# A decoder layer on one core: another order of the PSUM banks in the down projection, and a norm statistic and its squares moved in the opening

## The chip, the core and the metric

The kernel runs on one core of one Trainium2 chip. A core has a matrix engine (TensorE, PE in the profile, with its weight loads as PEld), a vector engine (VectorE, DVE), a scalar engine (ScalarE, ACT), a general engine (GpSimd, POOL) and a queue engine (SyncE, SP). Each engine takes its instructions in the order in which they stand in its queue. Matrix products are summed in PSUM, which has eight banks of 128 x 512 float32. The metric is the time of one execution on the device in microseconds (us).

## What is computed

One layer on x of 1024 tokens by 1024 features, all in float32:

```python
x = x + 0.5 * swiglu(rmsnorm(x, g1), gate1, up1, down1)   # (silu(h@gate) * (h@up)) @ down, width 2816
x = x + hybrid_mixer(rmsnorm(x, gm), ...)                 # gated linear attention and short convolutions
x = x + 0.5 * swiglu(rmsnorm(x, g2), gate2, up2, down2)
return rmsnorm(x, gf)
```

`rmsnorm` multiplies x by `rsqrt(mean(x*x) + eps)` and a gain.

## The kernel before

x lies in SBUF transposed: `xs[k]` holds 128 features by 1024 tokens, and the tokens are worked on in two halves of 512. Each float32 operand is split into a high and a low part (`split`: ScalarE casts, L92 or L557; VectorE subtracts, L85), and one product of two operands is three matrix instructions of 128 x 512, the `PASSES`. So "three instructions" below is one 128 x 128 block times 512 tokens.

Each SwiGLU (class `Ffn`) goes over 22 blocks of 128 of the inner width. `ups(f)` makes gate and up of block f for both halves at once by a seven product (Strassen) scheme; `down(g)` takes two such blocks, 2g and 2g+1, back to the 1024 features by seven products as well. The order of work is f = 4, 5, 6, ... with `down(g)` straight behind each even `ups(f)`, so a pair of `ups` with one `down` is 84 + 84 + 84 matrix instructions. There are 10 calls of `down` in each of the two SwiGLUs; the first call of the first one stands behind `ups(3)`, the 19 others behind an even `ups`.

PSUM banks are given out by number. An even `ups` uses banks 0 to 3 (`b = 4 * (f % 2)`): "a" is bank 0, "b" bank 1, "c" bank 2, "e" bank 3; an odd one uses banks 4 to 7. Bank 1 is read last by VectorE's product of silu(gate) and up (L701), bank 2 by ScalarE's silu of the last of the seven products (L705). `down` then writes its first product p = 1 for j = 0 to 3, three instructions each, into the four banks `a0[j]`, with copies by ScalarE into the banks `b0[j]` (L748):

```python
a0, b0 = [0, 3, 1, 2], [4, 7, 5, 6]
...
for j in range(4):
    if p == 1:
        av[j] = self.bank(a0[j])
        self.prod1(av[j], l4, r, True)
        bv[j] = self.bank(b0[j])
        S.copy(bv[j], av[j])
```

The last product of `down` (p = 4) sums into the same banks, and VectorE adds them to x for j = 0 to 3 (`xadd`, L715).

The first SwiGLU begins with `opening`, whose order is written by hand. `block(f, n, rights)` is gate and up of block f for half n, plain, in eight steps of six instructions; `some(b, m)` issues m steps of it. The first three blocks of half 0 are multiplied by x times gain, and the norm is applied after (`gated`: L536 and L537 on VectorE, silu L538 on ScalarE, L540 on VectorE). Half 1 is normed first. A `Norm` has `add(k)` (ScalarE squares x, L303, and VectorE adds to the sum, L88, one behind) and `fin`, a generator: its first `next` issues the statistic (L326: the sum times ones on TensorE, L337 on VectorE, a power L339 on GpSimd), its second the diagonal matrix `dg` (L343, VectorE), its third the broadcast by TensorE (L347) and ScalarE's copy of it to SBUF (`rb`, L351). `n0` and `n1` are the norms of the halves.

All instructions of a call keep the written order on TensorE; up to the first `down` they do so on all engines. Weights come by DMA from SP's queue some blocks ahead.

Of the kernel before, what the change touches and what calls it, by code (L numbers as in the profile page):

```python
# [19 lines left out]
KT = D // P  # L20
# [35 lines left out]
def trunk(ctx: ExitStack, tc: tile.TileContext, a, out):  # L56
# [22 lines left out]
    def t2(name):  # L79
        return room("t2", name)  # L80
# [6 lines left out]
    def add(eng, o, x, y):  # L87
        eng.tensor_tensor(o, x, y, op=ALU.add)  # L88
# [28 lines left out]
    def pump(n=None):  # L117
        while todo and n != 0:
            n = n and n - 1
            tag, step = todo[0]  # L120
            if not tag():
                return
            todo.popleft()
            step()

    def free(tag, n=1):
        used[tag] -= n
        assert used[tag] >= 0
# [116 lines left out]
    def tick(us):  # L245
        pump()
        clock[0] += us
        for e in list(later):
            if e[0] <= clock[0]:
                w = next(e[1], None)  # L250
                if w is None:
                    later.remove(e)
                else:
                    e[0] = clock[0] + w
# [16 lines left out]
    def xh(k, n):  # L271
        return xs[k][:, n * HALF:(n + 1) * HALF]
# [95 lines left out]
    def part_of(lt, j):  # L368
        return lt[:, j * P:(j + 1) * P], lt[:, 512 + j * P:512 + (j + 1) * P]
    class Ffn:  # L370
# [142 lines left out]
        def opening(self, n0, n1, load1):  # L513
# [7 lines left out]
            def some(b, n):  # L521
                for _ in range(n):
                    ps = next(b)
                return ps
# [7 lines left out]
            def gated(pss, n):  # L532

                o = t2("act")
                if n == 0:
                    V.tensor_tensor(o, pss[0], n0.r, op=ALU.mult)  # L536
                    V.tensor_tensor(pss[1], pss[1], n0.r, op=ALU.mult)  # L537
                S.activation(o, o if n == 0 else pss[0], AF.Silu)  # L538
                yield
                V.tensor_tensor(o, o, pss[1], op=ALU.mult)  # L540
                yield o
# [36 lines left out]
            a0 = self.block(0, 0, X)  # L578
# [9 lines left out]
            fin = n0.fin(self.bank_norm)  # L588
# [3 lines left out]
            some(a1, 2)  # L592
            n1.add(3)
            next(fin)
            n1.add(4)
            some(a1, 1)
            next(fin, None)
            for k in range(5, KT):
                n1.add(k)
            pump(6)  # L600
            act00 = gated(ps00, 0)
            next(act00)
            ps10 = some(a1, 2)
            fin = n1.fin(self.bank_norm)
            next(fin)
            act10 = gated(ps10, 0)
            a = [next(act00)]
            b = self.block(2, 0, X)
            some(b, 2)
            next(act10)  # L610
            next(fin)
            a.append(next(act10))
            some(b, 1)
            next(fin, None)
            ps20 = some(b, 5)

            self.right("R11", "R")
            for q in range(2):
# [115 lines left out]

        def down(self, g):

            a0, b0 = [0, 3, 1, 2], [4, 7, 5, 6]
            av, bv = {}, {}
            for n, p in enumerate(DOWN):
                lt, rt = self.left(("d", g), p), self.rights[n]  # L740
                r = [(rt[:, 0:512], rt[:, 512:1024])]
                for j in range(4):
                    l4 = part_of(lt, j)
# [5 lines that stand above are left out]
                    elif p == 2:  # L749
                        self.prod1(av[j], l4, r, False)  # L750
                        self.xadd(j, 0, av[j])
                    elif p == 6:
                        self.prod1(bv[j], l4, r, False)
                        av[j] = self.bank(a0[j])
                        S.copy(av[j], bv[j])
                    elif p == 3:
                        self.prod1(bv[j], l4, r, False)
                        self.xadd(4 + j, 0, bv[j])
                    elif p == 7:
                        self.prod1(av[j], l4, r, False)  # L760
                        self.xadd(4 + j, 1, av[j])
                    elif p == 5:
                        bv[j] = self.bank(b0[j])
                        self.prod1(bv[j], l4, r, True)
                        t = t2("dx")
                        S.mul(t, bv[j], 0.5)  # L766
                        for i in range(2):
                            add(G, xh(4 + j, i), xh(4 + j, i), t)
                    else:
                        self.prod1(av[j], l4, r, False)  # L770
                        self.xadd(j, 1, av[j])
                if n + 3 < len(DOWN):
                    self.rights[n + 3] = self.rights[n + 3]()
                free("wo")
                tick(2.72)
# [481 lines left out]
    n1 = [Norm(0, chain=V), Norm(HALF, chain=V)]  # L1257
# [200 lines left out]
```

## Time and profile before

| | |
|---|---|
| time, median of 3 executions | 1807.79 us (1807.17 to 1808.7) |
| the profiled execution's own time | 1805.88 us |
| its span in the profile | 1804.1 us |
| TensorE busy | 1741.6 us, 97% of the span |
| VectorE, ScalarE, GpSimd busy | 76%, 46%, 35% |
| mean granted TensorE clock | 0.986 |

The span reaches from the first to the last instruction of the profiled execution; 1.8 us of its time lie outside. The profiled execution was 1.9 us faster than the median of the three others. A granted clock of 1.00 is TensorE's level of 2.4 GHz, 0.50 that of 1.2 GHz.

### The profile page before, as it was taken

How to read it: one execution, taken by the hardware profiler on the slowest of the kernel's cores; microseconds unless marked ns; L12 is line 12 of the kernel's file. 1: busy time of each engine (PE TensorE's matmuls, PEld its weight loads, DVE VectorE, ACT ScalarE, POOL GpSimd, SP SyncE). 2: the span in 40 equal slices, each digit the busy share in tenths (PEclk: the TensorE clock that was granted, in tenths of full speed). 3: DMA queues.
4: the chain of work that ended last, by engine and by line, in shares of the span. 5: the costliest groups of instructions: out<-in, count | busy, mean ns of one | idle time of the engine just before them, and what ended most of it. 6: DMA issues, size and time to landing. Idle time of an engine off the chain costs nothing.

```text
span 1804.1 us, 21022 instructions
## 1 busy us (share of the span) xinstructions
PE 1741.6 (97%) x7814; PEld 1430.7 (79%) x7814; DVE 1373.1 (76%) x1847; ACT 831.0 (46%) x1442; POOL 627.6 (35%) x425
## 2 busy tenths in 40 slices
PE   8989999999999998899999999999999999999995
PEld 7768888888888875788888887888888888888884
DVE  6898778877798775775746678787788777977785
ACT  5465444554455444432352444454455544554453
POOL 0044254533444242220211021442545334442533
PEclk9999999999999998999999999999999999999997
DMA  5011212111111211222222223012121111112102
GB/s 213 1 47 47 71 47 71 47 48 62 55 47 47 71 53 47 82 82 82 72 92 83 82 71 101 17 36 70 48 70 48 47 60 58 47 47 70 47 24 94
DMA packets 35110, 112.92 MB, mean 63 GB/s; under 512 B 4384, under 2 KB 6848, under 8 KB 35008
## 3 DMA queue, kind: packets, MB, share of 16 engines
q1 hardware_dynamic: 32944, 108.42, 18.3%
q10 hardware_dynamic: 2064, 3.16, 0.5%
q8 instruction: 61, 1.00, 0.2%
q14 instruction: 41, 0.34, 0.1%
HBM read 107.37 MB, written 4.19 MB: 62 GB/s over the span
## 4 chain that ended last, share of the span: by engine, by line
PE 44%; issue 24%; POOL 17%; DVE 13%; ACT 2%; DMA 0%; POOLq 0%; ACTq 0%; DVEq 0%
PE ps L779 15%; POOL x L88 12%; PE pj L898 12%; PE dn L1203 5%; POOL raw L85 4%; DVE w L85 3%; PE ps L364 2%; PE v L953 2%; PE ps L799 2%; DVE S L85 2%; PE sc L1022 1%; DVE T L85 1%; DVE act L85 1%; PE ps L506 1%; DVE act L701 1%
## 5 line engine op out<-in xcount | busy, mean ns | idle before, releaser
L364 PE MATMUL ps<-R,w 128*128 128x512 f32 x1872 | 443.0, 390 | 3.4 <-DVE x L715 2.4
L364 PEld LDWEIGHTS ps<-R,w 128*128 128x128 f32 x1872 | 352.3, 188 | 77.9 <-DVE x L715 2.8
L779 PE MATMUL ps<-act,w 128*128 128x512 f32 x1680 | 390.0, 391 | 10.0 <-DVE act L701 9.3
L779 PEld LDWEIGHTS ps<-act,w 128*128 128x128 f32 x1680 | 313.7, 188 | 83.1 <-DVE act L701 17.3
L85 DVE TENSOR_TENSOR w<-raw,w 128x512 fp32r<-128x512 f32 x311 | 292.3, 946 | 78.8 <-ACT w L92 78.8
L364 PE MATMUL ps<-S,w 128*128 128x512 f32 x1404 | 331.3, 389 | 1.2 <-ACT w L92 1.2
L364 PEld LDWEIGHTS ps<-S,w 128*128 128x128 f32 x1404 | 263.4, 188 | 56.7 <-ACT w L92 1.7
L85 POOL TENSOR_TENSOR raw<-raw 128x512 f32<-128x512 f32 x59 | 77.3, 1310 | 608.0 <-DVE w L85 608.0
L88 POOL TENSOR_TENSOR x<-x,dx 128x512 f32<-128x512 f32 x160 | 265.7, 1697 | 17.4 <-ACT dx L766 17.4
L92 ACT CAST w<-raw 128x512 fp32r<-128x512 f32 x311 | 192.3, 620 | 167.3 <-POOL raw L85 75.9
L715 DVE SCALAR_TENSOR_TENSOR x<-ps,x 128x512 f32<-128x512 f32 x320 | 210.1, 682 | 33.7 <-PE ps L779 33.7
L898 PE MATMUL pj<-h,whi 128*128 128x512 f32 x640 | 200.4, 394 | 0.0
L85 DVE TENSOR_TENSOR wlo<-raw,whi 128x1024 fp32r<-128x1024 f32 x64 | 80.8, 1263 | 88.8 <-PE pj L898 47.4
L898 PEld LDWEIGHTS pj<-h,whi 128*128 128x128 f32 x640 | 118.9, 189 | 26.4 <-issue 1.9
L218 ACT CAST whi<-raw 128x1024 fp32r<-128x1024 f32 x64 | 67.0, 1047 | 138.7 <-PE pj L898 81.8
L85 DVE TENSOR_TENSOR w<-T,w 128x512 fp32r<-128x512 f32 x118 | 102.4, 868 | 37.1 <-ACT w L92 37.1
L898 PE MATMUL pj<-h,wlo 128*128 128x512 f32 x320 | 124.9, 390 | 0.0
L85 DVE TENSOR_TENSOR act<-act,act 128x512 fp32r<-128x512 f32 x103 | 109.9, 1069 | 13.1 <-ACT act L92 13.1
L92 ACT CAST act<-act 128x512 fp32r<-128x512 f32 x103 | 63.8, 622 | 75.1 <-PE ps L779 45.9
L92 ACT CAST w<-T 128x512 fp32r<-128x512 f32 x118 | 73.4, 622 | 53.5 <-PE ps L364 32.0
L85 POOL TENSOR_TENSOR raw<-raw,raw 128x512 f32<-128x512 f32 x59 | 95.6, 1620 | 4.6
L85 DVE TENSOR_TENSOR T<-raw,raw 128x512 f32<-128x512 f32 x59 | 49.6, 840 | 53.0 <-POOL raw L85 53.0
(196 smaller groups left out, 2150.7 us busy)
## 6 DMA issues: line engine op xcount, KB each, us to landing
raw<-in_ffn_w SPq DMA_DIRECT2D x86, 512.0 KB, 3.5
raw<-in_ffn_wd SPq DMA_DIRECT2D x44, 512.0 KB, 3.6
raw<-in_w_fm SPq DMA_DIRECT2D x40, 512.0 KB, 3.5
raw<-in_w_out SPq DMA_DIRECT2D x16, 512.0 KB, 3.5
x<-in_x SPq DMA_DIRECT2D x16, 256.0 KB, 6.4
raw<-in_w_v SPq DMA_DIRECT2D x8, 512.0 KB, 3.6
raw<-in_ffn_w ACTq DMA_DIRECT2D x2, 512.0 KB, 6.1
out<-y SPq DMA_DIRECT2D x2, 512.0 KB, 2.8
```

Of the source, the lines that this page charges most:

```text
L85: eng.tensor_tensor(o, x, y, op=ALU.subtract)
L88: eng.tensor_tensor(o, x, y, op=ALU.add)
L92: S.copy(hi, src)
L218: S.copy(st[1], st[0])
L364: nc.tensor.matmul(ps, lt[:, c:c + P], rk[j], start=(start and n == 0), stop=(n == last), skip_group_check=True)
L506: nc.tensor.matmul(pss[m], lts[m][:, c:c + P], rk[j], start=(q == 0 and k == 0 and t == 0), stop=(q == 1 and k == 3 and t == 2))
L715: V.scalar_tensor_tensor(xh(d, n), ps, 0.5, xh(d, n), op0=ALU.mult, op1=ALU.add)
L779: nc.tensor.matmul(ps, l2[i], r[0][j], start=(start and n == 0), stop=(n == 2), skip_group_check=True)
L799: nc.tensor.matmul(ps, l2[i], rts[h][q][:, 512 * j + o:512 * j + o + w], start=(q == 0 and k == 0), stop=(q == 1 and k == 2))
L898: nc.tensor.matmul(pss[f], w[i][:, k, f * P:(f + 1) * P], h[j][:, 4 * kh + k, :], start=(kh == 0 and k == 0 and n == 0), stop=(kh == 1 and ...
L953: nc.tensor.matmul(pss[t], h[i][:, kk, t * P:(t + 1) * P], u[j][:, k * 512:(k + 1) * 512], start=(kk == 0 and i == 0 and j == 0), stop=(kk ...
L1203: nc.tensor.matmul(pss[j], w[p][:, f * 512 + j * P:f * 512 + (j + 1) * P], act[q][i][:, f * 512:(f + 1) * 512], start=(i == 0 and f == 0 a ...
```

## The change

Two edits. `down` takes its four banks of gate and up in the order 0, 3, 2, 1. In the opening the squares 4 to 7 of half 1 are issued ahead of the broadcast of half 0's norm, the statistic of half 1 comes behind the first step of block 2 and behind the first `gated` result, and the broadcast of half 1 comes three steps before the end of block 2.

```diff
             next(fin)
-            n1.add(4)
+            for k in range(4, KT):
+                n1.add(k)
             some(a1, 1)
             next(fin, None)
-            for k in range(5, KT):
-                n1.add(k)
             pump(6)
             act00 = gated(ps00, 0)
             next(act00)
             ps10 = some(a1, 2)
-            fin = n1.fin(self.bank_norm)
-            next(fin)
             act10 = gated(ps10, 0)
             a = [next(act00)]
             b = self.block(2, 0, X)
+            some(b, 1)
+            fin = n1.fin(self.bank_norm)
+            next(fin)
             some(b, 2)
             next(act10)
             next(fin)
             a.append(next(act10))
-            some(b, 1)
+            some(b, 2)
             next(fin, None)
-            ps20 = some(b, 5)
+            ps20 = some(b, 3)
...
-            a0, b0 = [0, 3, 1, 2], [4, 7, 5, 6]
+            a0, b0 = [0, 3, 2, 1], [4, 7, 5, 6]
```

On TensorE, at the end of block 1 (`ps_229`, `ps_230`) and in block 2 (`ps_355`, `ps_356`), there stood before (a row is one instruction or several alike; `sq_116` is the sum of half 1's squares):

```order
L506 MATMUL ps_230<-S_4_114,S_16_224 128x512 x3
L326 MATMUL ps_345<-ones,sq_116 128x2 x4
L506 MATMUL ps_355<-S_3_113,L_319 128x512 x3
L506 MATMUL ps_356<-S_3_113,L_319 128x512 x3
L506 MATMUL ps_355<-S_3_113,L_319 128x512 x3
L506 MATMUL ps_356<-S_3_113,L_319 128x512 x3
L506 MATMUL ps_355<-S_3_113,L_319 128x512 x3
L506 MATMUL ps_356<-S_3_113,L_319 128x512 x3
L347 MATMUL ps_382<-dg_373,ones 128x512
```

At the same place of TensorE's queue stands now (block 2 is `ps_345`, `ps_346`):

```order
L506 MATMUL ps_230<-S_4_114,S_16_224 128x512 x3
L506 MATMUL ps_345<-S_3_113,L_319 128x512 x3
L506 MATMUL ps_346<-S_3_113,L_319 128x512 x3
L326 MATMUL ps_354<-ones,sq_116 128x2 x4
L506 MATMUL ps_345<-S_3_113,L_319 128x512 x3
L506 MATMUL ps_346<-S_3_113,L_319 128x512 x3
L506 MATMUL ps_345<-S_3_113,L_319 128x512 x3
L506 MATMUL ps_346<-S_3_113,L_319 128x512 x3
L506 MATMUL ps_345<-S_3_113,L_319 128x512 x3
L506 MATMUL ps_346<-S_3_113,L_319 128x512 x3
L506 MATMUL ps_345<-S_4_114,L_319 128x512 x3
L506 MATMUL ps_346<-S_4_114,L_319 128x512 x3
L347 MATMUL ps_394<-dg_379,ones 128x512
```

Six instructions of block 2 moved ahead of the statistic, and 24 instead of 18 stand between the statistic and the broadcast; 18 instead of 30 are left behind it. The profile counts twice as many instructions for L326 and L347, 8 and 2.

On ScalarE, around the copy `rb` of half 0's broadcast (`L_319` is block 2's weights):

```order
 L303 ACTIVATE sq_116<-x_82 128x512
-L351 COPY rb_307<-ps_305 128x512
 L303 ACTIVATE sq_116<-x_83 128x512
 L303 ACTIVATE sq_116<-x_84 128x512
 L303 ACTIVATE sq_116<-x_85 128x512
+L351 COPY rb_313<-ps_311 128x512
 L92 CAST L_319<-raw_315 128x512 x2
 L92 CAST L_319<-raw_317 128x512 x2
```

Three squares stand ahead of the copy now, and block 2's casts come right behind it. On VectorE the first `gated`'s L540 now stands ahead of the last addition to the sum (L88) instead of behind the statistic.

On TensorE, in the p = 1 of a `down` behind an even `ups` (`ps_1199` is j = 1, `ps_1205` j = 2, `ps_1211` j = 3), with what the first instruction of each group waits for:

```order
 L779 MATMUL ps_1199<-act_1110,w_1101 128x512 x3
-L779 MATMUL ps_1205<-act_1110,w_1101 128x512 [waits DVE_49]
+L779 MATMUL ps_1205<-act_1110,w_1101 128x512 [waits Activation_49]
 L779 MATMUL ps_1205<-act_1110,w_1101 128x512 x2
-L779 MATMUL ps_1211<-act_1110,w_1101 128x512 [waits Activation_49]
+L779 MATMUL ps_1211<-act_1110,w_1101 128x512 [waits DVE_49]
 L779 MATMUL ps_1211<-act_1110,w_1101 128x512 x2
```

The wait for VectorE moved from j = 2 to j = 3, and that for ScalarE from j = 3 to j = 2. SP's queue is the same, word for word.

## Rows read from the trace of the kernel before

**Rows 1.** The page: engine, busy us, share, instructions, for TensorE

```profile
PE 1741.6 (97%) x7814; PEld 1430.7 (79%) x7814; DVE 1373.1 (76%) x1847; ACT 831.0 (46%) x1442; POOL 627.6 (35%) x425
```

**Rows 2.** TensorE's waits, whole span: us in total, times, longest us

```profile
PE ps L779 <- DVE act L701: 9.3, 19, 0.5
```

**Rows 3.** TensorE timeline (start us, us, ...), end of an even ups, its down

```profile
321.16 5.60 PE L364 MATMUL ps<-R,w 128*128 128x512 f32 x24
326.60 1.52 PE L779 MATMUL ps<-act,w 128*128 128x512 f32 x6
328.61 17.97 PE L779 MATMUL ps<-act,w 128*128 128x512 f32 x78 [0.49 <-DVE act L701]
346.42 2.88 PE L364 MATMUL ps<-R,w 128*128 128x512 f32 x12
```

**Rows 4.** Timeline of VectorE, start of the same down

```profile
327.88 0.68 DVE L701 TENSOR_TENSOR act<-act,ps 128x512 f32<-128x512 f32 x1
...
330.98 0.69 DVE L715 SCALAR_TENSOR_TENSOR x<-ps,x 128x512 f32<-128x512 f32 x1 [1.22 <-PE ps L779]
```

**Rows 5.** Timeline of ScalarE, start of the same down

```profile
326.80 0.60 ACT L705 ACTIVATE sg<-ps 128x512 f32<-128x512 f32 x1 [0.57 <-PE ps L364]
```

**Rows 6.** Timeline of TensorE in the opening, 22 to 60 us

```profile
23.34 0.95 PE L326 MATMUL ps<-ones,sq 128*128 128x2 f32 x8
...
28.84 3.32 PE L506 MATMUL ps<-S,S 128*128 128x512 f32 x12
36.58 1.55 PE L326 MATMUL ps<-ones,sq 128*128 128x2 f32 x8 [4.43 <-DVE sq L88]
38.00 7.04 PE L506 MATMUL ps<-S,L 128*128 128x512 f32 x18
44.88 1.02 PE L347 MATMUL ps<-dg,ones 128*128 128x512 f32 x2
45.33 7.41 PE L506 MATMUL ps<-S,L 128*128 128x512 f32 x30
...
53.22 5.51 PE L506 MATMUL ps<-R,w 128*128 128x512 f32 x23 [0.23 <-DVE R L85]
59.09 0.50 PE L506 MATMUL ps<-R,w 128*128 128x512 f32 x1 [0.36 <-ACT R L557]
```

**Rows 7.** Timeline of ScalarE in the opening, 29 to 46 us

```profile
29.44 0.59 ACT L351 COPY rb<-ps 128x512 f32<-128x512 f32 x1 [7.07 <-PE ps L347]
29.92 1.68 ACT L303 ACTIVATE sq<-x 128x512 f32<-128x512 f32 x3
31.50 2.17 ACT L92 CAST L<-raw 128x512 fp32r<-128x512 f32 x4
...
45.93 0.59 ACT L351 COPY rb<-ps 128x512 f32<-128x512 f32 x1 [5.72 <-PE ps L347]
```

**Rows 8.** Timeline of VectorE in the opening, 30 to 37 us

```profile
32.14 2.50 DVE L85 TENSOR_TENSOR L<-raw,L 128x512 fp32r<-128x512 f32 x4
34.55 0.68 DVE L536 TENSOR_TENSOR act<-ps,rb 128x512 f32<-128x512 f32 x1
...
35.75 0.68 DVE L88 TENSOR_TENSOR sq<-sq 128x512 f32<-128x512 f32 x1
```

**Rows 9.** Two stretches: length, PE, PEld, DVE, ACT, POOL busy, then granted clock

```profile
36.50:43.70 7.20, 7.12 (x22) 5.89 (x23) 4.49 (x8) 0.63 (x1) 1.01 (x1) 0.53 0.17 65
132.50:135.90 3.40, 3.40 (x10) 2.67 (x8) 3.40 (x4) 0.00 (x0) 3.40 (x4) 0.50 0.00 0
```

**Rows 10.** Timelines of TensorE, VectorE, ScalarE at ups(4), 130 to 142 us

```profile
132.15 4.59 PE L364 MATMUL ps<-R,w 128*128 128x512 f32 x12 [2.40 <-DVE x L715]
...
139.30 2.88 PE L364 MATMUL ps<-R,w 128*128 128x512 f32 x12
...
137.71 0.68 DVE L715 SCALAR_TENSOR_TENSOR x<-ps,x 128x512 f32<-128x512 f32 x1
...
136.78 0.57 ACT L682 COPY ps<-ps 128x512 f32<-128x512 f32 x1 [6.32 <-PE ps L364]
```

## The prediction

> **What bounds the kernel now.** I read the page first: TensorE is busy 97% of the span [rows 1], so only its pauses and its slow stretches can be won. The list of its waits comes next, and one line is repeated: 19 times it stands before `down` for VectorE's L701, 9.3 us in all [rows 2]. The 19 are the calls of `down` behind an even `ups`. The timeline of one such call [rows 3] shows the place: after the first six instructions (j = 0 and 1), at the first of j = 2. Then I looked at the opening, where the longest single pause stands, 4.43 us at the statistic of half 1 [rows 6], and at the granted clock behind it [rows 9].
>
> **The order of banks.** In the rows the 24 instructions from 321.16 to 326.60 are 0.227 us apart. The 84 of `down` take from 326.60 to 346.42, 19.82 us, where 84 x 0.227 is 19.04 [rows 3]. So a call loses 0.78 us, more than the 0.49 us listed: the listed idle begins only at the modelled end of the sixth instruction. By spacing, the seventh was due at 326.60 + 6 x 0.227 = 327.96 and came at 328.61, 0.65 late; the remaining 0.13 is lost right after the restart or spread over the call.
>
> The Trainium skill ("TensorE: Matmul & The Clock Gate", Part 2, step 1) says that the next weights load while a product runs. By that a restart would cost nothing and a call would lose the 0.65 alone; the row's 0.78 includes what the restart takes, and I go by the row.
>
> Bank 1 comes free when L701 ends, 327.88 + 0.68 = 328.56, and TensorE starts 0.05 later [rows 3, 4]. Bank 2 is free when the silu L705 ends, 326.80 + 0.60 = 327.40 [rows 5], 0.56 before 327.96. With 0, 3, 2, 1 the group j = 2 runs from 327.96 without a pause. Group j = 3 is due at 326.60 + 9 x 0.227 = 328.64, and bank 1 is ready for it at 328.61. The margin is 0.03 us. The weights of an instruction load ahead of it and carry the wait, so I charge 0.1 of the 0.13 again. That leaves 0.68 us a call, 19 x 0.68 = **12.9 us**. Bounds: 0.78 x 19 = 14.8 if nothing is left, and 0.55 x 19 = 10.5 if L701 lands 0.13 later against TensorE.
>
> What is late next: the copies L748 and the adds L715 follow the products. VectorE idles 1.22 us for TensorE before the first L715 of this call [rows 4]; TensorE's 0.68 comes out of that pause and leaves 0.5. Without that cover VectorE would set the pace from there. No instruction is added in `down`, and SP's queue is unchanged, so the DMAs only move with the buffers.
>
> The first `down` of the first SwiGLU stands behind `ups(3)`, which uses the other four banks: no gain there. But `ups(4)` comes right behind it and copies its first product into bank 1 (L682). That bank now belongs to j = 3, whose add ends last, at 137.71 + 0.68 = 138.39, while the copy ran at 136.78 and takes 0.57 [rows 10]. The copy would end at 139.0. TensorE needs it for its third product, which began at 139.30. So it costs nothing as the trace stands. The cover is the half clock: the 12 instructions at 132.15 took 4.59 us at a granted clock of 0.50 [rows 9, 10] instead of some 2.9. Without that slow stretch the third product would be due some 1.7 sooner, at 137.6, and the new copy would hold it by up to 1.4 us. I take 0, bounds 0 and +1.4.
>
> **The opening.** Before, ScalarE stood 7.07 us for TensorE ahead of the copy `rb` at 29.44; three squares (1.68 us) and block 2's casts came after it [rows 7]. Now the squares run in that pause and the casts start at 29.92 instead of 31.50, 1.58 earlier. VectorE's four subtractions follow cast by cast, so L536 moves from 34.55 to 32.97. Between it and the last addition to the sum stood L537 (34.55 to 35.75 is two steps of 0.60 [rows 8]); now L540 stands there too, 0.6 and some 0.2 of waiting for the silu. The last addition starts at 32.97 + 1.2 + 0.8 = 34.95 instead of 35.75, and the statistic, 0.83 behind it [rows 6, 8], at 35.8 instead of 36.58.
>
> TensorE finishes block 1 at 28.84 + 3.32 = 32.16 [rows 6], now runs six more instructions until 33.5, and idles 2.3 us instead of 4.43. Then: statistic 0.95, 24 instructions (5.4 at 0.227), broadcast; `rb` starts 1.05 after it (44.88 to 45.93 [rows 6, 7]). At full clock that is 43.2, against 45.93: -2.7 us.
>
> The clock decides. After the 4.43 us pause the granted clock was 0.53 from 36.5 to 43.7, and the 18 instructions at 38.00 took 6.88 us to the next row instead of 4.1 [rows 6, 9]. After the 2.40 us pause before 132.15 it was 0.50 for 3.4 us, and 12 instructions lost 1.7 [rows 9, 10]. A pause of 2.3 is nearest to the second, so I take 1.7 lost here: `rb` at 44.9, -1.0.
>
> Behind the broadcast 18 instructions are left instead of 30, 12 x 0.227 = 2.7 us less cover. But block (0,1) needs half 1's normed operand, which VectorE and ScalarE make after `rb`, and for which TensorE already waited 0.23 at 53.22 [rows 6], 7.3 after `rb`. So TensorE will idle some 2.7 us anew before that block: block 2's saved time is not kept, and the block's start moves with `rb` alone. After such a pause the clock may fall again: 1.7 lost, of which the waits at 53.22 and 59.09 (0.6 [rows 6]) and a like one behind them absorb some 0.7. So +1.0, and the opening nets **0**. Bounds: -2.7 (clock stays full in both pauses), +2.5 (`rb` 0.5 later than before, since six more instructions run at half rate, and 2.0 behind the second pause).
>
> **Sum.** -12.9 + 0 + 0 = -12.9. Against the profiled execution, 1805.88, that is 1793.0; the median of the three shown is 1.9 higher. I apply the difference to the median: **1794.9 us**.
>
> **Rivals.**
> 1. The clock stays full over both shorter pauses. For: 2.3 is half of 4.43. Against: the 2.40 us pause before 132.15. Time 1807.8 - 12.9 - 2.7 = 1792.2. The same page of the Trainium skill (Part 1) has the clock at half by default and activity releasing it, which speaks for shorter pauses; no run shown has this one.
> 2. The opening loses: half clock in both, 24 instructions under it, and perhaps the held copy in `ups(4)`. 1794.9 + 2.5 = 1797.4, with 1.4 more 1798.8. For: the statistic itself is hardly work and prolongs the slow stretch, 1.55 instead of 0.95 [rows 6]. Against: idle is shorter than before.
> 3. The wait for bank 1 stays in half at j = 3, because L701 lands 0.34 later against TensorE's products: 19 x 0.34 given up, 1801.3. The margin of 0.03 speaks for it; against it, VectorE runs through from the products of the `ups` to L701 in all 19 calls alike (the longest wait is 0.5, and 9.3 / 19 is 0.49 [rows 2]).
> 4. L701 lands 0.7 or more later: the wait has only changed its place, 1807.8, no change.
> 5. Slower: bank 2 is late. L705 stands in ScalarE's queue among casts and copies. If it fell behind three instructions of its own length, 1.8 us, it would end at 329.2, 0.64 after bank 1 is free today: 19 x 0.64 more, 1820. It decides from the point where L705 ends after 328.56; today it ends 1.16 before [rows 4, 5], and the change keeps the order of ScalarE's queue there.
>
> **Chances.** Forecast 0.50 (its own range 1793 to 1797), rival 1 0.17, rival 2 0.19, rival 3 0.07, rival 4 0.05, rival 5 0.02. The range from 1790.5 to 1799.5 takes in rivals 1 and 2 with the upper bound of the banks (14.8), and leaves out rivals 3 to 5 and some of the edges. A measurement of this kernel tells about 0.2%, 3.6 us, from no change: faster 0.93, the same 0.05, slower 0.02.
>
> **What would show it.** In the profile after: the line L779 <- L701 gone or below 0.1 us a call, a pair of `ups` and its `down` 0.7 us shorter, no line L779 <- ACT L705; the statistic of half 1 at 35.8 after a pause of 2.3; a new pause of 2 to 3 us before block (0,1); the second `rb` between 43.2 and 46.4; L682 of `ups(4)` waiting for L715. I would be wrong if L701's distance to the products moves with the pace, or if the clock behaves otherwise after 2.3 us than after 2.40.

## The result and the profile after

| | before | after |
|---|---|---|
| time, median on the same chip | 1808.24 us (4 executions, 1807.17 to 1808.77) | 1793.67 us (4 executions, 1791.72 to 1794.18) |
| ratio, 95% interval | | 0.9918 (0.9906 to 0.993) |
| the profiled execution's own time | 1805.88 us | 1794.18 us |
| its span | 1804.1 us | 1792.4 us |
| mean granted TensorE clock | 0.986 | 0.983 |

The kernel is faster by 14.6 us, where 12.9 were forecast; the 1793.67 lie 1.2 below the forecast 1794.9 and inside the range. Three signs of the forecast are looked up first: the wait, the pair, the opening.

The first view of the changed kernel is the list of TensorE's waits (us in all, times, longest). The line L779 <- L701, 9.3 us in 19 waits before [rows 2], is not among its lines any more; of `down` it still has one wait of 0.7, and two lines of 2.5 and 2.4 us are to be looked at below:

```profile
PE ps L326 <- DVE sq L88: 14.1, 6, 4.1
...
PE ps L506 <- ACT R L557: 2.5, 1, 2.5
PE ps L364 <- DVE x L715: 2.4, 1, 2.4
...
PE ps L779 <- DVE x L715: 0.7, 1, 0.7
```

The same list of the weight loads (PEld) has the nineteen, with what is left of them, 0.23 us each:

```profile
PEld ps L779 <- DVE act L701: 4.4, 19, 0.2
```

TensorE's timeline (start, duration, engine, line, operation, tiles, shape, count) shows the same call as [rows 3]. The 84 instructions of `down` stand in one row without a pause and take from 326.12 to 345.26, 19.14 us; before they took 19.82:

```profile
320.68 5.60 PE L364 MATMUL ps<-R,w 128*128 128x512 f32 x24
326.12 19.30 PE L779 MATMUL ps<-act,w 128*128 128x512 f32 x84
345.26 2.88 PE L364 MATMUL ps<-R,w 128*128 128x512 f32 x12
```

VectorE's timeline of that call is the answer to [rows 4]. L701 ends at 327.40 + 0.68 = 328.08, and group j = 3 is due at 326.12 + 9 x 0.227 = 328.16: bank 1 is ready 0.08 us ahead. The pause before the first L715 has shrunk from 1.22 to 0.54, so VectorE still waits for TensorE there and not the reverse:

```profile
327.40 0.68 DVE L701 TENSOR_TENSOR act<-act,ps 128x512 f32<-128x512 f32 x1
...
329.82 0.69 DVE L715 SCALAR_TENSOR_TENSOR x<-ps,x 128x512 f32<-128x512 f32 x1 [0.54 <-PE ps L779]
```

The opening on TensorE, beside [rows 6]. The pause before the statistic is 2.31 instead of 4.43, the 24 products behind it take 8.05 us to the next row, where 24 x 0.227 is 5.4, and a new pause of 2.48 stands before block (0,1):

```profile
28.70 3.32 PE L506 MATMUL ps<-S,S 128*128 128x512 f32 x12
31.86 1.52 PE L506 MATMUL ps<-S,L 128*128 128x512 f32 x6
35.69 1.76 PE L326 MATMUL ps<-ones,sq 128*128 128x2 f32 x8 [2.31 <-DVE sq L88]
37.30 8.21 PE L506 MATMUL ps<-S,L 128*128 128x512 f32 x24
45.35 1.02 PE L347 MATMUL ps<-dg,ones 128*128 128x512 f32 x2
45.81 4.68 PE L506 MATMUL ps<-S,L 128*128 128x512 f32 x18
52.97 12.90 PE L506 MATMUL ps<-R,w 128*128 128x512 f32 x48 [2.48 <-ACT R L557]
```

On ScalarE (two views, the first casts of block 2 and the second `rb`) the casts begin at 29.79 and the copy `rb` at 46.41, against 31.50 and 45.93 [rows 7]:

```profile
29.79 2.18 ACT L92 CAST L<-raw 128x512 fp32r<-128x512 f32 x4
...
46.41 0.59 ACT L351 COPY rb<-ps 128x512 f32<-128x512 f32 x1 [7.51 <-PE ps L347]
```

The windows of three stretches (length, then busy us of PE, PEld, DVE, ACT and POOL, the granted clock, the DMA share, GB/s) answer to [rows 9]. The clock is at its lower level, 1.2 GHz, behind each of the three pauses: behind the statistic, at the start of block (0,1), and in `ups(4)`:

```profile
35.80:42.60 6.80, 6.80 (x21) 5.64 (x22) 3.91 (x7) 0.63 (x1) 1.01 (x1) 0.50 0.08 33
52.90:56.20 3.30, 3.23 (x7) 2.33 (x8) 3.22 (x5) 1.84 (x4) 0.00 (x0) 0.50 0.00 0
131.30:138.20 6.90, 5.50 (x13) 4.35 (x14) 6.90 (x7) 0.00 (x0) 6.48 (x5) 0.51 0.00 0
```

Last, `ups(4)` on TensorE and on ScalarE, beside [rows 10]. The twelve products took 5.49 us instead of 4.59, the low stretch being longer here, and the copy L682 ran at 138.97 instead of 136.78, straight behind the last L715. It ended at 139.54, ahead of the third product at 140.85:

```profile
132.70 5.49 PE L364 MATMUL ps<-R,w 128*128 128x512 f32 x12 [2.39 <-DVE x L715]
137.99 3.02 PE L364 MATMUL ps<-S,w 128*128 128x512 f32 x12
140.85 2.88 PE L364 MATMUL ps<-R,w 128*128 128x512 f32 x12
```

```profile
138.97 0.57 ACT L682 COPY ps<-ps 128x512 f32<-128x512 f32 x1
```

**Where the time went.** The two profiled executions are 11.7 us apart. I took the start of each `down` on TensorE in both and subtracted. Eight pairs of the first SwiGLU (from the second call to the tenth) take 457.76 us instead of 463.20, nine of the second 514.96 instead of 521.12: 11.60 us over 17 calls, 0.68 each. The two calls left make 1.36, so 19 calls are 12.96. Against that stand +0.55 at the start of `ups(3)` (87.47 instead of 86.92) and +1.01 from there to the second `down` (66.98 instead of 65.97), where the half clock in `ups(4)` lasted longer; the rest, -0.3, is spread over the mixer and the end. The medians differ by 2.9 us more than the profiles: the profiled execution of before was 2.4 us under its median of 1808.24, and that of after 0.5 over its own.

### The profile page after: what moved, and what is told of

It is laid out like the page before. It is cut to its first block, busy times and chain, and to the rows that moved or that the text cites. A ratio compares the mean times of both kernels' runs of the same rounds, so it can differ in the third digit from the quotient of the medians.

```text
span 1792.4 us, 21018 instructions
## 1 busy us (share of the span) xinstructions
PE 1740.0 (97%) x7814; PEld 1432.2 (80%) x7814; DVE 1373.2 (77%) x1847; ACT 830.8 (46%) x1442; POOL 627.3 (35%) x425
## 4 chain that ended last, share of the span: by engine, by line
PE 89%; issue 5%; DVE 4%; ACT 1%; POOL 1%; DMA 0%; ACTq 0%; POOLq 0%; DVEq 0%
PE ps L364 41%; PE ps L779 20%; PE pj L898 12%; PE dn L1203 5%; PE ps L482 2%; PE v L953 2%; PE ps L799 2%; PE sc L1022 1%; PE ps L506 1%; DVE sq L88 1%; PE alr L916 0%; DVE x L715 0%; DVE hraw L355 0%; DVE act L85 0%; DVE x L802 0%
## 5 line engine op out<-in xcount | busy, mean ns | idle before, releaser
L779 PE MATMUL ps<-act,w 128*128 128x512 f32 x1680 | 386.3, 390 | 0.7 <-DVE x L715 0.7
L779 PEld LDWEIGHTS ps<-act,w 128*128 128x128 f32 x1680 | 313.7, 188 | 70.1 <-DVE act L701 4.4
L88 POOL TENSOR_TENSOR x<-x,dx 128x512 f32<-128x512 f32 x160 | 265.7, 1697 | 17.5 <-ACT dx L766 17.5
L715 DVE SCALAR_TENSOR_TENSOR x<-ps,x 128x512 f32<-128x512 f32 x320 | 210.2, 682 | 20.7 <-PE ps L779 20.7
```

The source lines that it names most:

```text
L715: V.scalar_tensor_tensor(xh(d, n), ps, 0.5, xh(d, n), op0=ALU.mult, op1=ALU.add)
L779: nc.tensor.matmul(ps, l2[i], r[0][j], start=(start and n == 0), stop=(n == 2), skip_group_check=True)
```

## The experiments

My theory was that of the prediction: the gain is the wait for bank 1, paid 19 times and priced by how late L701 comes against TensorE's products, and the opening gives nothing. The rival, fed by the 14.6 us that were more than 12.9: a part of the gain comes from the opening. Each kernel ran beside the kernel before on its chip.

**The order of banks alone** (on the kernel before):

```diff
-            a0, b0 = [0, 3, 1, 2], [4, 7, 5, 6]
+            a0, b0 = [0, 3, 2, 1], [4, 7, 5, 6]
```

> The kernel before with the bank order 0, 3, 2, 1 alone; the opening is the old one. Theory A (the 19 calls of down give 0.68 us each, the opening about nothing): 12.9 us off, 1795.3 us; a pair of ups with its down 57.2 us long instead of 57.9; no wait of L779 for L701 in the list of waits. Theory B (a part of the gain is the opening's, by its shorter pause): only 10 us off, about 1798. Under both, the copy of ups(4) into bank 1 ends at about 139.0.

It took 1795.06 us (1793.42 to 1795.65, 5 executions) against 1809.47 (1805.83 to 1811.58, 17): ratio 0.992 (0.9908 to 0.9932), 14.4 us. In TensorE's timeline two successive calls of `down` start 57.21 us apart, which is 252 x 0.227:

```profile
267.39 19.29 PE L779 MATMUL ps<-act,w 128*128 128x512 f32 x84
...
324.60 19.30 PE L779 MATMUL ps<-act,w 128*128 128x512 f32 x84
```

This edit alone gives the whole gain, within the intervals. The copy of `ups(4)` ended at 138.46 + 0.57 = 139.03, 0.31 ahead of the third product at 139.34; the forecast had 139.0 and 139.30:

```profile
138.46 0.57 ACT L682 COPY ps<-ps 128x512 f32<-128x512 f32 x1 [0.98 <-DVE x L715]
```

**The opening alone** (the changed kernel with the old order of banks):

```diff
-            a0, b0 = [0, 3, 2, 1], [4, 7, 5, 6]
+            a0, b0 = [0, 3, 1, 2], [4, 7, 5, 6]
```

> The changed opening with the old bank order 0, 3, 1, 2. Theory A: the opening nets between -1 and +1 us, 1808.2 us and no difference that can be told; 19 waits of 0.49 us for L701 stand as before; a pause of 2.3 us before the statistic, one of 2.5 before block (0,1), a low clock behind both. Theory B: 2 to 3 us faster than before, 1805.5.

It took 1807.91 us (1803.69 to 1812.93, 12) against 1809.47: ratio 0.9994 (0.9985 to 1.0004), no difference that can be told. The interval reaches to 2.7 us of gain, so by itself it does not exclude the lower end of the rival's 2 to 3 us; but the banks alone took off as much as both edits together, so nothing of the 14.6 us calls for the opening. The 19 waits are back, on TensorE and on its weight loads:

```profile
PE ps L779 <- DVE act L701: 9.2, 19, 0.5
```

```profile
PEld ps L779 <- DVE act L701: 17.3, 19, 0.9
```

The second line, which the list of the kernel before has word for word too, shows how the loss is best read: 17.3 - 4.4 = 12.9 us, 0.68 a call, which is what the pairs gained. TensorE's own 9.2 falls short of it by 3.7. In the opening of this execution the pause was the same as in the changed kernel's, 2.30, but the half clock lasted only 3.4 us, and the 24 products took 7.17 us to the next row instead of 8.05:

```profile
36.14 1.02 PE L326 MATMUL ps<-ones,sq 128*128 128x2 f32 x8 [2.30 <-DVE sq L88]
37.03 7.34 PE L506 MATMUL ps<-S,L 128*128 128x512 f32 x24
```

**Banks and squares, statistic and broadcast at the old places** (on the kernel before, with the new order of banks):

```diff
-            n1.add(4)
+            for k in range(4, KT):
+                n1.add(k)
             some(a1, 1)
             next(fin, None)
-            for k in range(5, KT):
-                n1.add(k)
```

> New bank order, and of the opening only the squares 4 to 7 of half 1 moved ahead of the broadcast; statistic and broadcast of half 1 stand at the old places. Theory A (what counts in the opening is when rb of half 1 is copied, and six instructions between statistic and broadcast fewer help it): the statistic at 35.0, 18 instructions at half rate for most of them, rb at 44.4, block (0,1) at 51.3 without a long pause: 0.9 us faster than the new banks alone, 1794.4. Rival (the opening is hidden anyway): 1795.3, as the new banks alone.

It took 1794.89 us (1794.68 to 1796.61, 5): ratio 0.9921 (0.9909 to 0.9934), as with the banks alone. Its opening ran 2.5 us later than before (the statistic of half 0 at 25.84, not 23.34): the granted clock was 0.50 from 10.0 to 13.4 us, where it had been 1.00. Counted from that statistic, the statistic of half 1 came 1.56 us earlier than before, after a pause of 2.86. The banks again give the whole of it; what the squares win in the opening is too small for the time to show.

**Bank 1 second**, so that the same wait comes one group earlier than in the kernel before:

```diff
-            a0, b0 = [0, 3, 2, 1], [4, 7, 5, 6]
+            a0, b0 = [0, 1, 3, 2], [4, 7, 5, 6]
```

> The changed kernel with the bank order 0, 1, 3, 2: bank 1 is wanted by the second group of each down. Theory A (a down waits for bank 1 until L701 ends, and only how late it is wanted matters): the second group is due 0.68 us after the first and starts when L701 ends, 2.0 after; 1.33 plus 0.13 of restart lost in each of 19 calls instead of 0.1, 25.8 us more than the changed kernel: 1819. A pair of ups with its down 58.6 us. Rival E (VectorE sets the pace of a pair, the place of the wait is only its symptom): as before the change, 1808.

It took 1823.37 us (1820.62 to 1828.44, 4) against 1809.77 (1806.29 to 1811.97, 7): ratio 1.0071 (1.0053 to 1.0088). The waits grew to 1.17 us each on TensorE and 1.59 on the weight loads, and the pair in the timeline grew to 410.76 - 352.16 = 58.60 us, 0.70 more than before and 1.39 more than with the wait gone:

```profile
PE ps L779 <- DVE act L701: 22.2, 19, 1.2
```

```profile
PEld ps L779 <- DVE act L701: 30.2, 19, 1.6
```

```profile
331.64 0.84 PE L779 MATMUL ps<-act,w 128*128 128x512 f32 x3
333.65 18.67 PE L779 MATMUL ps<-act,w 128*128 128x512 f32 x81 [1.17 <-DVE act L701]
352.16 2.88 PE L364 MATMUL ps<-R,w 128*128 128x512 f32 x12
...
410.76 1.52 PE L364 MATMUL ps<-R,w 128*128 128x512 f32 x6
```

One group of three earlier costs 3 x 0.227 = 0.68 us more a call, so the price is the lateness, to 0.02 us a call. The 1823.37 lie 4 us over the 1819 expected; against the kernel before beside it the loss is 13.6 us, and 19 x 0.70 is 13.3. By the weight loads: 30.2 - 4.4 = 25.8 us, 1.36 a call.

**Bank 2 second**, so that the silu L705 is asked for 0.68 us sooner:

```diff
-            a0, b0 = [0, 3, 2, 1], [4, 7, 5, 6]
+            a0, b0 = [0, 2, 3, 1], [4, 7, 5, 6]
```

> The changed kernel with the bank order 0, 2, 3, 1: the bank that ScalarE's silu L705 reads is wanted by the second group, 0.68 us after the first. Theory A: L705 ends 0.80 after the first group's start, so the wait has a new releaser: L779 waits for L705, 0.15 to 0.2 us of start and 0.1 of restart lost a call, 0.2 more than the changed kernel: 3.8 us, 1797.5; no wait for L701, since bank 1 is wanted last and later still. Rival (only VectorE's bank matters): 1793.7.

It took 1800.2 us (1798.49 to 1804.29, 4) against 1809.77: ratio 0.9951 (0.9934 to 0.9968). TensorE's list of waits has no line for it; the list of its weight loads has:

```profile
PEld ps L779 <- ACT sg L705: 8.3, 19, 0.5
```

```profile
265.39 19.55 PE L779 MATMUL ps<-act,w 128*128 128x512 f32 x84
...
322.85 19.55 PE L779 MATMUL ps<-act,w 128*128 128x512 f32 x84
```

The pair is 57.46 us, 0.25 longer than 57.21, and (8.3 - 4.4) / 19 is 0.21: 4 to 5 us in all, 6 by the two ratios (expected 3.8). A wait that TensorE's row does not show (84 in one row) still costs. The opening of this execution is the third way that the clock can go: the same pause of 2.31, and full clock behind it. The broadcast came 6.47 us after the statistic and not 9.66:

```profile
35.83 1.02 PE L326 MATMUL ps<-ones,sq 128*128 128x2 f32 x8 [2.31 <-DVE sq L88]
36.71 5.75 PE L506 MATMUL ps<-S,L 128*128 128x512 f32 x24
42.30 1.02 PE L347 MATMUL ps<-dg,ones 128*128 128x512 f32 x2
```

```profile
35.80:45.00 9.20, 9.17 (x42) 7.39 (x43) 4.41 (x8) 2.26 (x4) 1.01 (x1) 1.00 0.07 30
```

**Statistic one step later, broadcast two steps behind it** (on the changed kernel):

```diff
-            some(b, 1)
+            some(b, 2)
             fin = n1.fin(self.bank_norm)
             next(fin)
             some(b, 2)
             next(act10)
             next(fin)
             a.append(next(act10))
-            some(b, 2)
             next(fin, None)
-            ps20 = some(b, 3)
+            ps20 = some(b, 4)
```

> The changed kernel with the statistic of half 1 behind two steps of block 2 instead of one, and its broadcast two steps (12 instructions) behind it instead of four (24). Theory A (the pause of 2.3 us lowers the clock, and the start of block (0,1) hangs on rb): the pause before the statistic is 1.1 us, the clock stays full, rb at 40.4, a pause of about 1.6 before block (0,1) at 47, 6 us sooner than after the change: 1788. Rival C (the clock falls after any pause here): rb at 42.5, block (0,1) at 49, 1790 to 1791. Rival D (block (0,1) does not hang on rb): no faster than the changed kernel, 1793.7.

It took 1788.83 us (1788.0 to 1789.9, 4) against 1809.47: ratio 0.9888 (0.9875 to 0.9901). The statistic keeps its time, the pause before it is filled down to 0.94, the clock stays full, the broadcast comes 3.72 us behind the statistic, and block (0,1) starts at 47.12 instead of 52.97:

```profile
31.95 2.88 PE L506 MATMUL ps<-S,L 128*128 128x512 f32 x12
35.78 1.02 PE L326 MATMUL ps<-ones,sq 128*128 128x2 f32 x8 [0.94 <-DVE sq L88]
36.66 3.00 PE L506 MATMUL ps<-S,L 128*128 128x512 f32 x12
39.50 1.02 PE L347 MATMUL ps<-dg,ones 128*128 128x512 f32 x2
39.96 6.04 PE L506 MATMUL ps<-S,L 128*128 128x512 f32 x24
47.12 0.50 PE L506 MATMUL ps<-R,w 128*128 128x512 f32 x1 [1.12 <-ACT R L557]
```

**Only the broadcast earlier** (the statistic where the change put it):

```diff
             a.append(next(act10))
-            some(b, 2)
             next(fin, None)
-            ps20 = some(b, 3)
+            ps20 = some(b, 5)
```

> The changed kernel with the broadcast of half 1 two steps (12 instructions) behind the statistic instead of four, and the statistic left behind one step. Theory A: the pause of 2.3 us stays, and the clock behind it is low for 3.4 or 6.8 us as in the changed kernel; rb at 43 to 43.6; block (0,1) at 49.5 to 50.2 without a pause of its own, since 30 instructions stand behind the broadcast: about 2.5 us less than the changed kernel, 1791.2, and 2.4 more than e4, which has the same distance but no low clock. Rival (the length of the first pause does not matter, only the distance to the broadcast): as e4, 1788.8.

It took 1791.3 us (1790.64 to 1791.8, 4) against 1809.77: ratio 0.9898 (0.9883 to 0.9913). The pause before the statistic stays at 2.31, the half clock behind it lasts 3.4 us, and no wait is left at the first product of block (0,1): with 12 products between statistic and broadcast instead of 24, the operand of half 1 is there in time. The opening alone had the same pause, the same 3.4 us and the wait of 2.48, so the place of the broadcast made that wait.

**The later statistic, with half 0's operand split ahead of the broadcast** (on the kernel of the later statistic), so that ScalarE and VectorE are through with it when `rb` comes:

```diff
             a.append(next(act10))
-            next(fin, None)
-            ps20 = some(b, 4)
-
             self.right("R11", "R")
...
             parts("R11", lambda k: raws[0, k], lambda k: n0.raw(raws[0, k], self.g, k))
+            next(fin, None)
+            ps20 = some(b, 4)
```

> The kernel of e4 with the operand R11 made ahead of the broadcast of half 1: VectorE and ScalarE split it in the pause that they have until rb, instead of behind rb and ahead of block (0,1)'s operand. Theory A (block (0,1) hangs on the chain rb, R11, R12): rb as in e4 or up to 1 us later, since ScalarE's casts stand ahead of it, block (0,1) at 46.0 to 46.7 instead of 47.1, the wait before it 0.2 or less; 0.5 to 1.1 us less than e4, 1787.7 to 1788.3. Rival (the chain is bound by VectorE's whole work, R11 included): as e4, 1788.8, the wait moves into block (0,1).

It took 1791.09 us (1787.74 to 1792.42, 4) against 1809.77: ratio 0.9894 (0.9879 to 0.991), some 3 us over the time expected. The pause before block (0,1) is gone, but the clock fell for 3.4 us although the pause before the statistic was only 0.95. By its time it can't be told apart from the kernel without the earlier split.

**The later statistic once more**, the same kernel in other executions:

> The kernel of e4 once more, on the same chip as e10. Theory A: the opening as in e4 up to the clock, 0.989 of the kernel before, 1788 to 1790.

It took 1791.42 us (1787.53 to 1793.9, 5) against 1807.88 (1805.82 to 1810.56, 9): ratio 0.9904 (0.989 to 0.9918), over the 1788 to 1790 expected. Here too the clock fell behind a pause of 0.95. And in `ups(4)` it did not fall: the window from 128.4 to 135.3 has 1.00. Without that cover TensorE was held by the copy (L681 is the changed kernel's L682, one line up), as the prediction's upper bound had it. The third product was due at 131.32 + 12 x 0.227 = 134.04 and came at 135.39, 1.35 late:

```profile
131.32 2.88 PE L364 MATMUL ps<-S,w 128*128 128x512 f32 x12
135.39 3.06 PE L364 MATMUL ps<-R,w 128*128 128x512 f32 x12 [1.19 <-ACT ps L681]
```

```profile
128.40:135.30 6.90, 5.74 (x24) 4.43 (x24) 6.90 (x9) 1.16 (x3) 5.18 (x4) 1.00 0.00 0
```

From `ups(3)` to the second `down` it still took 65.89 us, against 65.97 before: what the full clock won, the copy took.

**The split ahead of the broadcast, and the old order in the first call alone**, so that the copy of `ups(4)` is not held:

```diff
-            a0, b0 = [0, 3, 2, 1], [4, 7, 5, 6]
+            a0, b0 = [0, 3, 1, 2] if (self.i, g) == (1, 0) else [0, 3, 2, 1], [4, 7, 5, 6]
```

> The kernel of e7 with the old bank order 0, 3, 1, 2 in the first call of down alone, so that the copy of ups(4) into bank 1 need not wait for the last add. Theory A: the copy runs as soon as the first product is done, but TensorE's third product is not held by it in any run so far, so nothing is gained there while the clock is low behind the pause before ups(4) (20.8 us from the start of ups(4) to the start of its down, as in e1); block (0,1) earlier than in e4 by what e7 showed, 1 us; 1787 to 1789, and 0 to 2 us under e9. Rival (the copy does hold TensorE): from the start of ups(4) to its down 19.5 to 20.2 us, 1786.

It took 1789.56 us (1788.2 to 1793.8, 4) against 1807.88: ratio 0.9905 (0.989 to 0.9919), a little over the 1787 to 1789 expected. The stretch from `ups(3)` to the second `down` is 66.00 us with the clock low in `ups(4)`, and 66.01 in the kernel without this line: nothing gained while the clock is low there. Whether it saves the 1.35 us where the clock stays full, no run showed.

**The openings together.** One profiled execution each. The second column is the pause before the statistic of half 1, the third the length at granted clock 0.50 behind it (from slices of 0.5 us), the fourth the wait at the first product of block (0,1), the last two the starts of half 1's `rb` and of `ups(3)`. Both are counted from the statistic of half 0, since in three executions (squares moved too, bank 1 second, broadcast earlier) 3.4 us of half clock ahead of it put off everything by 1.6 to 2.9 us.

| kernel | pause | half clock | wait at block (0,1) | `rb` | `ups(3)` |
|---|---|---|---|---|---|
| before | 4.43 | 6.8 | none | 22.59 | 63.58 |
| banks alone | 4.42 | 6.8 | none | 22.58 | 63.60 |
| squares moved too | 2.86 | 6.8 | none | 20.93 | 61.92 |
| changed kernel | 2.31 | 6.8 | 2.48 | 23.21 | 64.27 |
| opening alone | 2.30 | 3.4 | 2.48 | 21.59 | 62.61 |
| bank 1 second | 2.31 | 3.4 | 2.48 | 21.62 | 62.66 |
| bank 2 second | 2.31 | none | 2.48 | 20.02 | 61.05 |
| broadcast earlier | 2.31 | 3.4 | none | 18.86 | 59.86 |
| statistic later | 0.94 | none | 1.12 | 17.26 | 58.28 |
| statistic later, again | 0.95 | 3.4 | 1.14 | 18.86 | 59.89 |
| split first | 0.95 | 3.4 | none | 20.65 | 57.28 |
| split first, old order in the first call | 0.95 | 3.4 | none | 20.64 | 57.27 |

Rows four to seven have the same opening and differ by 3.2 us through the clock alone. In the first ten rows `ups(3)` begins 41.0 us after `rb`, whatever the waits and the clock between them (40.99 to 41.06); with the split first it is 36.6. And at the same half clock of 3.4 us "broadcast earlier" and "statistic later, again" have the same `rb`: the six more products ahead of the statistic gave nothing there. What both gain from is what they share: 12 products instead of 24 between statistic and broadcast.

## Why the prediction was right

**The banks, -12.9.** Right in mechanism and size: 0.68 us a call measured, 0.68 forecast, and a pair 0.68 to 0.69 shorter. The 0.10 a call that I left in is there too (19.14 against 19.04), and it stands where I put it, at the weights. In this call the weights of a product begin to load some 0.22 us ahead of it (325.90 and 326.12 at the first). Those of the first product of j = 3 (due at 327.94) waited for bank 1 and began at 328.13, 0.05 after L701's end:

```profile
325.90 2.00 PEld L779 LDWEIGHTS ps<-act,w 128*128 128x128 f32 x9
328.13 16.87 PEld L779 LDWEIGHTS ps<-act,w 128*128 128x128 f32 x75 [0.23 <-DVE act L701]
```

The product itself came when it was due, at 328.16, but the next one at 328.47 instead of 328.39, 0.08 late (TensorE's timeline from 328.64 to 328.70); the four behind it lost 0.02 more:

```profile
328.47 0.40 PE L779 MATMUL ps<-act,w 128*128 128x512 f32 x1
```

In the kernel before, the first product after the pause began at 328.61 and the next at 328.94, 0.11 later than the spacing of 0.227 has it (timeline from 329.11 to 329.17), and 0.02 followed there too:

```profile
328.94 0.40 PE L779 MATMUL ps<-act,w 128*128 128x512 f32 x1
```

So the 0.13 beside the lateness is lost right after the restart and not spread over the call. With the pause of 1.17 us it is 0.15 (352.16 - 331.64 = 20.52, less 19.04, less 1.33 of lateness). The rule that I set against the row (the Trainium skill, "TensorE: Matmul & The Clock Gate", Part 2, step 1: the next weights load while a product runs) fits the products that wait for nothing. At a bank that is late the weights wait as well, and the restart costs 0.13 to 0.15 us, not nothing.

**Bank 2, and rivals 3 to 5.** Bank 2 was in time as forecast: no line L779 <- L705 stands in either list of the changed kernel. L701 kept its place against the products, so neither half nor all of the wait came back, though the margin was 0.08 us. The two other orders show such waits at work: 0.25 us a call for bank 2, 1.39 for bank 1.

**The opening, 0.** Right in sum: 0.9994 (0.9985 to 1.0004) for it alone. Its steps: the casts at 29.79 (forecast 29.92), the statistic at 35.69 after 2.31 (35.8 after 2.3; the 34.95 on the way to it is 34.97 by its own terms), the pause before block (0,1) 2.48 (some 2.7).

But two terms of the sum were wrong. The first is the half clock behind the first pause: the 24 products lost 8.05 - 5.4 = 2.6 us in the profiled execution, and the statistic 0.7 (37.30 - 35.69 = 1.61, against 36.71 - 35.83 = 0.88 at full clock in bank 2 second), where I had taken 1.7 in all. So `rb` came at 46.41, at my upper bound, and not at 44.9. The second is the +1.0 for half clock behind the second pause, and it did not exist. From `rb` to `ups(3)` it is 41.06 us in the changed kernel and 41.04 in bank 1 second, where the clock fell there, 41.02 and 41.03 in the opening alone and bank 2 second, where it did not, and 40.99 before. In block (0,1) TensorE waits for operands at full clock (0.23, 0.36 and 0.23 us before); with the half clock it does not (48 products in one row from 52.97), so the lower clock costs nothing there. That `ups(3)` began only 0.55 late, near the 0, was luck: the first term was 1.5 us too cheap, the second 1.0 too dear.

The step that was too simple is the sentence that lets the clock decide once: I read one length of the low stretch from the nearest pause. The executions show three outcomes behind one pause. Rival 1's clock is that of bank 2 second, 2.5 us earlier than before (its price 2.7). Rival 2's half clock in both pauses is that of the changed kernel and of bank 1 second, at +0.7 and -0.9 (its price +2.5). Over the four that have this opening, `rb` comes 1.0 us and `ups(3)` 0.9 us earlier than before in the mean, too little to be seen in the time.

**The held copy, 0.** The cover was the half clock, as the step said: with it L682 ended 0.31 us ahead of need with the banks alone and 1.3 in the changed kernel, whose half clock was longer; without it the third product was 1.35 late, forecast up to 1.4. I had not seen that the two cancel: where the clock stays full, the 1.7 us that it wins pay for the copy.

**The 1.7 us between forecast and result.** They come from no term: the profiles differ by 11.7 us, less than 12.9. The forecast applied a difference worked out from one execution to medians, and the kernel before varies from 1805.8 to 1812 us by itself. Its time goes with the mean granted clock: of 17 executions beside the first experiments, three took 1805.8 to 1806.0 us at 0.985 or 0.986, the others 1809.3 to 1811.6 at 0.980 to 0.983. The profiled execution of before was one at 0.986, that of after one at 0.983, so the two profiles show too little. A part of this spread lies where the change edits nothing: from 660 to 745 us, at the end of the first SwiGLU and the start of the mixer, the granted clock was 0.92 in the profile of before and 0.86 in that of the banks alone, and from the tenth `down` to the eleventh they took 574.56 and 576.45 us, although the second saves 0.68 on the way. Of the four executions of after one was at 0.986 too; it took 1791.72, 14.2 less than 1805.88. The last 1.3 us of that over 12.9 stay open.

**A version that may be faster still.** The later statistic took 0.9888 and 0.9904 of the kernel before in two runs, the changed kernel 0.9918: 2.5 to 5.4 us less. The first interval lies clear of the changed kernel's, the second overlaps it, so it is likely and not settled. The earlier broadcast (0.9898) and the variants with the split ahead of the broadcast (0.9894, 0.9905) are not told apart from it.

## What to carry to other kernels

Give out the banks in the order in which their last readers end, and price a bank that is late by its lateness at its place in the queue, times the calls; moving it one group moved the price by 0.70 us a call, and the group lasts 0.68. Read the loss from the length of a whole period or from the waits of the weight loads, since the list of TensorE's own waits had 9.2 of 12.9 us of it in one kernel and nothing in another. Ask of filler ahead of a statistic what it does to the way from the statistic to its broadcast: with 24 products between them the filled pause came back before the next block, with 12 it did not or only in part. Here all that followed hung on `rb`, and `ups(3)` came 41.0 us behind it at either clock.

## What the runs showed of the chip that I had not expected

The same pause of 2.31 us before the statistic was followed by half clock for 6.8 us, for 3.4 us, or not at all, and even 0.95 us was followed by 3.4 us of it in three executions out of four. The Trainium skill ("TensorE: Matmul & The Clock Gate", Part 1, "What's actually happening") says that the number of products run at half clock at the start of a kernel varies from run to run. Here the later statistic, one kernel, varies so in its middle: no half clock behind the pause in one execution and 3.4 us in another. What decides between the outcomes the runs don't tell. The statistic itself, eight products of two columns, stands between pause and filler in each of these cases, and no run took it away. But the pause of 2.4 us at `ups(4)` has no statistic, and there too the clock fell in eleven profiled executions out of twelve, for 3.4 us in nine and 6.8 in two.

A wait that is listed on PEld alone, with TensorE's products in one unbroken row, cost 0.25 us a call (bank 2 second), and the 0.23 us that are left in the changed kernel cost 0.10.
